# First expert layer: expert rows added to the tokens by indirect accumulating DMA in DRAM in place of one-hot products

## The chip, the cores and the metric

The kernel runs on one core of a Trainium2 chip. The metric is the device time of one execution in microseconds (us), and the median of several runs counts. A core has TensorE (PE, with its weight loads shown apart as PEld), VectorE (DVE), ScalarE (ACT), GpSimd (POOL) and SyncE (SP). DMAs are issued here from SP's and POOL's queues.

## The reference, cut to what matters

512 tokens of width 1024 (and 256 context tokens) go through a first block and then two layers, each a mixer followed by an expert layer with 16 experts. The change is in the first of the two expert layers, which serves both token sets. Every expert chooses its best tokens: 64 of the 512 tokens, 32 of the 256 context tokens. A token may be chosen by several experts, and their outputs are added.

```python
cap = max(1, EC_FACTOR * T // N_EXPERTS)              # 64 for tokens, 32 for the context
aff = softmax(h @ router)
gate, idx = lax.top_k(swapaxes(aff, 1, 2), cap)
xs = h[idx]
hid = silu(xs @ w1) * (xs @ w3)                       # per expert, 1024 x 1024 weights, float32
ys = (hid @ w2) * gate
out = zeros((T, D)).at[idx].add(ys)                   # x = x + g2 * out
```

## The kernel before

The function `moe` builds one expert layer. In the first layer it has two groups: group 0, the four token tiles of 128 x 1024 (`xres`), with 64 rows to an expert, and group 1, the two context tiles (`cres`), with 32 rows. 128 rows are handled together: two experts of group 0 (`ne` = 2), four of group 1 (`ne` = 4). So group 0 has 8 such bundles and group 1 has 4. The second expert layer has one group only (`alone`).

`choose` finds the chosen tokens on VectorE, eight at a time. `fetch` (L1479 to L1489) turns slot numbers into token numbers with one-hot products on TensorE: 4 of them for group 0 and 2 for group 1, each recorded as two instructions with 128 stationary columns. The token numbers (`ii`) drive an indirect gather on POOL's queue (L1483), which reads rows of the normalised tokens `xh` from DRAM into `xs`. `turn` (L1573 to L1579) transposes them.

`run` loops over the 16 experts. Of an expert, `up` (L1623) multiplies the rows of group 0 (`h`) and group 1 (`hc`) with w1 and w3, `act` and `turned` (L1630 to L1646) apply the gate and transpose, `down` (L1662) multiplies with w2 (`yb`), and `collect` (L1675 to L1680) puts the rows into `ys`. Twelve weight tiles of 1 MB serve one expert; 14 of them fit, and each is loaded on SP's queue (L1464) when the tile that held its place is free.

When a bundle's last expert is done, `scatter` is put into the list `beside`. Its steps run during the next expert: two of them between quarters of `up`, the rest after `act` of group 0. So group 0's scatter runs during experts 2, 4, 6, ... 14, group 1's during experts 4, 8 and 12, and the last scatter of each group after expert 15. `fetch` for the next bundle of group 0 stands in experts 0, 2, ... 12, that for group 1 in 2, 6 and 10, and `turn` an expert later.

A scatter of this layer scales the 128 rows by the gate on ACT (L1594, `yh` in a reduced matmul type, with the remainder `yl` from DVE, L1596). For every token tile it builds a one-hot matrix `back` on DVE (L1600), multiplies it with both halves of `yh` and `yl` on TensorE (L1605), and adds the product to the tile on DVE (L1607). That is 16 products for group 0, 8 for group 1. Group 1's rows are multiplied by the modulation gate on POOL first (L1593).

The order of instructions on each engine is fixed when the kernel is built, by a planner that follows the program order as a priority and its own estimates of times. Every engine runs its instructions in that order; a DMA's wait stands on the queue of the engine that issues it.

Of the kernel before, what the change touches and what calls it, by code (L numbers as in the profile page):

```python
# [10 lines left out]
F32 = mybir.dt.float32  # L11
F32R = mybir.dt.float32r
BF16 = mybir.dt.bfloat16
I32 = mybir.dt.int32
AF = mybir.ActivationFunctionType
ALU = mybir.AluOpType
# [4 lines left out]
D = 1024  # L21
# [1416 lines left out]
def moe(k, layer, groups, mods, psum, es, nslot, extra, out=None, side="right"):  # L1438
# [4 lines left out]
    nc, I = k.nc, k.i  # L1443
    bank = lambda nm="ps": psum.tile([128, 512], F32, name=nm, tag="ps")
    dp = k.pool(f"md{layer}", 1, DRAM, es)
    parts = [("w1", 0), ("w3", 0), ("w1", 1), ("w3", 1), ("w1", 2), ("w3", 2), ("w1", 3), ("w3", 3), ("w2", 0), ("w2", 1), ("w2", 2), ("w2", 3)]
    todo = [(e, nm, q) for e in range(16) for nm, q in parts]
    W, pools, G, made = {}, [], [], {}

    alone = len(groups) == 1  # L1450

    def slots():

        if not pools:
            pools.append(k.pool(f"mw{layer}", 1, None, es, side))
        return lambda: pools[0].tile([128, 2 * D], F32, name="w", tag="w", bufs=nslot)

    def load(upto, eng=nc.sync):

        for i in range(len(W), min(upto, len(todo))):  # L1460
            e, nm, q = todo[i]
            a = i % (nslot + extra) >= nslot
            w = pools[a].tile([128, 2 * D], F32, name="w", tag="w", bufs=extra if a else nslot).rearrange("p (k f) -> p k f", k=2)
            d = eng.dma_start(w, I[f"moe_{nm}_2"][layer, e][q * 256:q * 256 + 256].rearrange("(k p) f -> p k f", p=128))  # L1464
            if i < nslot + extra:
                k.tc.keep_in_program_order(d)
            W[e, nm, q] = w

    def fetch(g, gi, a):

        n, ne, cap = g["n"], g["ne"], g["cap"]
        b = bank()
        w = 1 if alone else n
        for t in range(0, n, w):
            oh = pf.tile([128, w, ne, cap], F32, name="oh", tag=f"oh{gi}", bufs=1 + alone)
            nc.vector.tensor_tensor(oh, iota[:, :cap].unsqueeze(1).unsqueeze(1).to_broadcast([128, w, ne, cap]),
                                    g["pos"][:, t:t + w, a * ne:a * ne + ne].unsqueeze(3).to_broadcast([128, w, ne, cap]), op=ALU.is_equal)
            for i in range(w):
                nc.tensor.matmul(b[:, :ne + 1], oh[:, i].rearrange("p e c -> p (e c)"), g["ext"][:, t + i, a], start=(t + i == 0), stop=(t + i == n - 1))  # L1479
        ii = pf.tile([128, 1], I32, name="ii", tag=f"ii{gi}", bufs=2)  # L1480
        nc.vector.tensor_copy(ii, b[:, 0:1])
        xs = pf.tile([128, D], F32, name="xs", tag="xs", bufs=len(groups))
        nc.gpsimd.indirect_dma_start(out=xs, out_offset=None, in_=g["xh"][:, :],  # L1483
                                     in_offset=bass.IndirectOffsetOnAxis(ap=ii[:, 0:1], axis=0))
        sl = pf.tile([128, ne + 1], F32, name="sl", tag=f"sl{gi}", bufs=2)
        nc.vector.tensor_copy(sl, b[:, :ne + 1])  # L1486
        gate = pf.tile([128, 1], F32, name="gt", tag=f"gt{gi}", bufs=2)
        for e in range(ne):
            nc.vector.tensor_scalar(gate[e * cap:e * cap + cap], sl[e * cap:e * cap + cap, 1 + e:2 + e], 0.5, None, ALU.mult)  # L1489
        return dict(xs=xs, sl=sl, gate=gate)  # L1490

    def begin(p):

# [87 lines left out]
    def scatter(g, c, last):  # L1581

        ys = c["ys"]
        last = last and out is not None
        dt = F32 if alone else F32R
        if alone:
            terms = [ys]
        else:
            terms = [p.tile([128, D], F32R, name=nm, tag=nm, bufs=1) for nm in ("yh", "yl")]
        pieces = [slice(0, 512), slice(512, 1024)] if last else [slice(0, D)]  # L1590
        for cs in pieces:
            if g["cap"] == 32:
                nc.gpsimd.tensor_tensor(ys, ys, g["gate"], op=ALU.mult)  # L1593
            nc.scalar.activation(terms[0][:, cs], ys[:, cs], AF.Copy, scale=c["gate"])  # L1594
            if not alone:
                nc.vector.scalar_tensor_tensor(terms[1][:, cs], ys[:, cs], c["gate"], terms[0][:, cs].bitcast(F32), ALU.mult, ALU.subtract)  # L1596
            yield
            for t in range(g["n"]):
                back = pf.tile([128, 128], dt, name="back", tag="back", bufs=2)
                nc.vector.tensor_scalar(back, iota, 128.0 * t, c["sl"][:, 0:1], ALU.add, ALU.is_equal)  # L1600
                for o in range(cs.start, cs.stop, 512):
                    hs = slice(o, o + 512)
                    b = bank()
                    for i, y in enumerate(terms):
                        nc.tensor.matmul(b, back, y[:, hs], start=(i == 0), stop=(i == len(terms) - 1))  # L1605
                    x = g["tiles"][t][:, hs]
                    nc.vector.tensor_tensor(x, x, b, op=ALU.add)  # L1607
                    if last:
                        nc.sync.dma_start(out[t * 128:t * 128 + 128, hs], x)
                if t % 2:  # L1610
                    yield
# [70 lines left out]
    def run():  # L1682
        nonlocal rp, pf, pq, p, iota, tid, one, hb
        slots()
        rp = k.pool(f"mr{layer}", 1, None, es)
        iota = rp.tile([128, 128], F32, name="iota")
        nc.gpsimd.iota(iota, pattern=[[1, 128]], base=0, channel_multiplier=0, allow_small_or_imprecise_dtypes=True)
        tid = rp.tile([128, 6], F32, name="tid")
        nc.gpsimd.iota(tid, pattern=[[128, 6]], base=0, channel_multiplier=1, allow_small_or_imprecise_dtypes=True)
        for gi, g in enumerate(G):  # L1690
            g["gate"] = mods.gate(g["r"], 1, rp, f"g2{layer}{gi}")
        if extra:
            pools.append(k.pool(f"mv{layer}", 1, None, es))
        load(nslot + extra - (2 if extra else 6))
        pf = k.pool(f"mf{layer}", 1, None, es)
        with ExitStack() as e2:
            pq = k.pool(f"mq{layer}", 1, None, e2, "left")
            one = pq.tile([16, 512], F32, name="one")
            nc.gpsimd.memset(one, 1.0)
            chosen = [choose(gi, g) for gi, g in enumerate(G)]  # L1700
            while any(g is None for g in nxt):
                for c in chosen:
                    next(c, 0)
        load(nslot + extra, nc.gpsimd)
        load(24)
        p = k.pool(f"mx{layer}", 1, None, es)
        for gi, g in enumerate(G):
            turn(g, gi, nxt[gi])
        for e in range(16):
            load(12 * e + 36)  # L1710
            for gi, g in enumerate(G):
                if e % g["ne"] == 0:
                    cur[gi] = nxt[gi]
            hb = [[bank("h1"), bank("h3")] if g["cap"] == 64 else [bank("hc")] for g in G]
            ybs, hTs, late = [bank("yb") for _ in G], [None] * len(G), len(G) - 1

            def ups(q, gi):
                if 0 <= q < 4:
                    up(e, q, gi, G[gi])

            def downs(q, gi):
                if 0 <= q < 4:
                    down(e, q, gi, G[gi], hTs[gi], ybs[gi])


            for q in range(4):
                ups(q, 0)
                if late:
                    ups(q - 1, 1)
                if q > 1:  # L1730
                    beside.step()
            th = act(0, G[0])
            beside.drain()
            for gi, g in enumerate(G):
                if e % g["ne"] == g["ne"] - 2 and e < 16 - 2:
                    nxt[gi] = fetch(g, gi, e // g["ne"] + 1)
            hTs[0] = turned(0, G[0], th)
            if late:
                ups(3, 1)
                th = act(1, G[1])  # L1740
            for q in range(4 + 2 * late):
                downs(q, 0)
                if late and q == 1:
                    hTs[1] = turned(1, G[1], th)
                if late:
                    downs(q - 2, 1)
                if q == 1:
                    for gi, g in enumerate(G):
                        if e % g["ne"] == g["ne"] - 1 and e < 15:
                            turn(g, gi, nxt[gi])  # L1750
            for gi, g in enumerate(G):
                collect(e, gi, g, ybs[gi])
                if e % g["ne"] == g["ne"] - 1:
                    beside.add(scatter(g, cur[gi], e == 15))
        beside.drain()
        es.close()
# [898 lines left out]
```

## Time and profile before

| | us |
|---|---|
| median of 3 runs | 3433.63 |
| lowest and highest | 3430.89, 3440.51 |
| the profiled execution's own time | 3434.85 |
| its span in the profile | 3432.6 |

The mean granted clock of TensorE over the span was 0.939 of full speed. PE was busy for 3083.4 us (90% of the span), DVE 1528.3, ACT 1014.2, POOL 976.9. The first expert layer's loop lies between 1497 and 2128 us of the span. What lies outside the span in the profiled execution is 2.25 us.

### The profile page before, as it was taken

Reading aid. Unit: us, or ns where it says so; the run is one execution under the profiler, and the core shown is the slowest. Engines: PE = TensorE matmul, PEld = TensorE weight load, DVE = VectorE, ACT = ScalarE, POOL = GpSimd, SP = SyncE. Lnnn points to the kernel's source line nnn. Section 1 sums busy time; section 2 is a strip of 40 time slices with the busy share of each in tenths; the row PEclk is TensorE's granted clock in tenths of the full one; section 3 lists DMA queues with packets and bytes.
Section 4 is the critical chain, followed back from the end, with each engine's and each line's share of the span. In section 5 each row is a group of like instructions: output and inputs, shape, how many; then the busy total and the mean of one; then the engine's idle time right before and its main releaser. Section 6 shows DMA issues by size and latency. Waiting matters only on the chain.

```text
span 3432.6 us, 52377 instructions
## 1 busy us (share of the span) xinstructions
PE 3083.4 (90%) x21072; PEld 2017.0 (59%) x21072; DVE 1528.3 (45%) x3435; ACT 1014.2 (30%) x2175; POOL 976.9 (28%) x859
## 2 busy tenths in 40 slices
PE   8999999999899889969999998899768579699888
PEld 6897878877668666833333333787547467333322
DVE  4324354423477786332323225321678776322212
ACT  4434333321213555211212112122647443011000
POOL 5342433433323561310000001424646343000000
PEclk9999999999999999979999999899879779799999
DMA  4121221235266331379888883343312234899998
GB/s 145 63 73 62 74 74 62 74 102 160 80 166 170 97 102 50 124 287 348 326 337 327 334 337 131 111 137 105 93 47 75 65 94 155 323 409 409 409 409 347
DMA packets 372551, 625.93 MB, mean 182 GB/s; under 512 B 43998, under 2 KB 240525, under 8 KB 372310
## 3 DMA queue, kind: packets, MB, share of 16 engines
q1 hardware_dynamic: 367190, 603.58, 49.3%
q0 software_dynamic: 5120, 19.01, 1.5%
q8 instruction: 166, 2.72, 0.3%
q14 instruction: 75, 0.61, 0.1%
HBM read 596.61 MB, written 25.91 MB: 181 GB/s over the span
## 4 chain that ended last, share of the span: by engine, by line
PE 73%; DVE 11%; DMA 8%; ACT 4%; issue 2%; POOL 2%; SPq 1%; DVEq 0%; ACTq 0%; POOLq 0%
PE ps L102 11%; PE h L1623 10%; PE ps L103 10%; PE ps L104 10%; PE yb L1662 7%; DMA w<-in_moe_w_dram 5%; PE hc L1623 4%; PE ps L1605 2%; PE ps L932 1%; PE ps L2259 1%; DVE pr L2314 1%; DVE acc L1106 1%; PE ob L1309 1%; DVE N L2315 1%; PE ps L1271 1%
## 5 line engine op out<-in xcount | busy, mean ns | idle before, releaser
L201 POOL TENSOR_TENSOR wlo<-wraw,whi 128x1024 fp32r<-128x1024 f32 (+5 forms) x219 | 426.0, 1967 | 734.0 <-ACT whi L197 708.9
L1623 PE MATMUL h<-w,xT 128*64 128x512 f32 x2048 | 463.8, 599 | 23.9 <-DMA w<-in_moe_w_dram 18.4
L1623 PEld LDWEIGHTS h<-w,xT 128*64 128x64 f32 x2048 | 141.3, 137 | 336.3 <-issue 254.1
L1662 PE MATMUL yb<-w,hT 128*64 128x512 f32 (+1 forms) x1536 | 301.6, 600 | 17.8 <-ACT hT L1646 15.4
L197 ACT CAST whi<-wraw 128x2048 fp32r<-128x2048 f32 (+4 forms) x108 | 161.7, 1497 | 233.0 <-PE ps L103 124.3
L1483 POOL DMA_INDIRECT xs<-xh,ii x20 | 21.4, 1069 | 733.4 <-DVE sl L1486 713.0
L1631 DVE SCALAR_TENSOR_TENSOR th<-th,h 128x512 f32<-128x512 f32 x32 | 22.0, 689 | 413.9 <-ACT th L1630 413.9
L1662 PEld LDWEIGHTS yb<-w,hT 128*64 128x64 f32 (+1 forms) x1536 | 87.3, 128 | 198.3 <-issue 155.7
L102 PE MATMUL ps<-hT,whi 128*128 128x512 f32 x416 | 171.2, 411 | 0.0
L102 PE MATMUL ps<-whi,hT 128*128 128x512 f32 (+1 forms) x424 | 163.3, 386 | 6.2 <-DVE hT L316 4.0
L1630 ACT ACTIVATE th<-h 128x512 f32<-128x512 f32 x32 | 19.1, 598 | 500.7 <-PE h L1623 500.7
L104 PE MATMUL ps<-hT,whi 128*128 128x512 f32 x416 | 166.1, 399 | 0.0
L103 PE MATMUL ps<-hT,wlo 128*128 128x512 f32 x416 | 166.1, 399 | 0.0
L103 PE MATMUL ps<-whi,hT 128*128 128x512 f32 (+1 forms) x424 | 155.7, 367 | 0.0
L104 PE MATMUL ps<-wlo,hT 128*128 128x512 f32 (+1 forms) x424 | 154.2, 366 | 0.0
L115 POOL TENSOR_TENSOR rs<-rs_t,mhalf 128x8 f32<-128x8 f32 (+3 forms) x78 | 96.0, 1235 | 119.2 <-DVE rs_t L110 99.6
L1675 DVE TENSOR_TENSOR ys<-yb,g 64x512 f32<-64x512 f32 x64 | 44.1, 689 | 180.2 <-PE yb L1662 179.6
L1623 PE MATMUL hc<-w,xT 128*32 128x512 f32 x1024 | 124.2, 598 | 0.0
L102 PEld LDWEIGHTS ps<-whi,hT 128*128 128x128 f32 x424 | 104.1, 246 | 15.7 <-DVE hT L316 4.3
L103 PEld LDWEIGHTS ps<-whi,hT 128*128 128x128 f32 x424 | 104.6, 247 | 6.5 <-issue 2.1
L1106 DVE SCALAR_TENSOR_TENSOR acc<-glu,w,acc 128x798 f32<-128x798 f32 x90 | 106.7, 1221 | 1.0
L104 PEld LDWEIGHTS ps<-wlo,hT 128*128 128x128 f32 x424 | 103.7, 245 | 5.4 <-issue 0.6
(810 smaller groups left out, 6787.7 us busy)
## 6 DMA issues: line engine op xcount, KB each, us to landing
w<-in_moe_w_dram SPq DMA_DIRECT2D x376, 1024.0 KB
wraw<-in_w_in_dram SPq DMA_DIRECT2D x48, 1024.0 KB
aw<-in_ada_w_dram SPq DMA_DIRECT2D x192, 256.0 KB
wraw<-in_od_w_in_dram SPq DMA_DIRECT2D x27, 512.0 KB
rows<-rw_rows SPq DMA_DIRECT2D x48, 192.0 KB
w<-in_moe_w_dram POOLq DMA_DIRECT2D x8, 1024.0 KB, 8.7
xh<-xn SPq DMA_DIRECT2D x10, 512.0 KB
wraw<-in_w_proj_b_dram SPq DMA_DIRECT2D x4, 1024.0 KB
```

The source lines that it names most:

```text
L102: nc.tensor.matmul(out, L[0], R[0], start=start, stop=False)
L103: nc.tensor.matmul(out, L[1], R[0], start=False, stop=False)
L104: nc.tensor.matmul(out, L[0], R[1], start=False, stop=stop)
L115: nc.gpsimd.tensor_tensor(out, t, mh.to_broadcast(list(ss.shape)), op=ALU.pow)
L197: nc.scalar.copy(hi, raw)
L201: eng.tensor_tensor(lo[:, a:b], raw[:, a:b], hi[:, a:b].bitcast(F32), op=ALU.subtract)
L932: nc.tensor.matmul(ps[32 * j:32 * j + 32, h * w:h * w + w], k.cT[:, 4 * q + j], raws[i][:, j], start=(q == 0), stop=(q == 1), tile_positio ...
L1106: v.scalar_tensor_tensor(acc[:, c], glu[:, c, j:j + W], w2[:, j, c:c + 1], acc[:, c], ALU.mult, ALU.add)
L1605: nc.tensor.matmul(b, back, y[:, hs], start=(i == 0), stop=(i == len(terms) - 1))
L1623: nc.tensor.matmul(bb[o:o + cap], lhs, w[:, kk % 2, fh * 512:fh * 512 + 512], start=(kk == 0), stop=(kk == 7), tile_position=(0, o))
L1662: nc.tensor.matmul(yb[o:o + cap], lhs, w[:, j, dh * 512:dh * 512 + 512], start=first, stop=last, tile_position=(0, o))
L1675: nc.vector.tensor_tensor(ys[so, ds_], yb[64 * dh:64 * dh + 64], g["gate"][so, ds_], op=ALU.mult)
```

## The change

In the first expert layer a copy of the tokens (`acc`, one per group) is written to DRAM when `run` begins, by six DMAs of 512 KB on SP's queue. `scatter` of every bundle but each group's last scales the rows once on ACT into a float32 tile `yd` (one buffer for both groups) and issues one indirect accumulating DMA per expert on POOL's queue, 64 or 32 rows of 4 KB each, which adds the rows to `acc` at the token numbers. When one bundle of a group is left, the tiles are read back from `acc` on SP's queue. The last bundle of each group goes back by one-hot products as before. An indirect DMA takes its row numbers from the first partitions on, so `fetch` makes the token numbers of a bundle's second and later experts once more, by further products with one column on the cap partitions, and copies them to `i2`.

```diff
@@ fetch
+            if not alone:
+                for e in range(1, ne):
+                    for i in range(n):
+                        nc.tensor.matmul(b[:cap, 8 + e:9 + e], oh[:, i, e], g["ext"][:, i, a, 0:1], start=(i == 0), stop=(i == n - 1))
-        ii = pf.tile([128, 1], I32, name="ii", tag=f"ii{gi}", bufs=2)
+        ii = pf.tile([128, 1], I32, name="ii", tag=f"ii{gi}", bufs=2 if alone else 3)
         nc.vector.tensor_copy(ii, b[:, 0:1])
+        own = [ii[:cap]]
+        if not alone:
+            i2 = pf.tile([cap, ne], I32, name="i2", tag=f"i2{gi}", bufs=3)
+            nc.vector.tensor_copy(i2[:, 1:], b[:cap, 9:8 + ne])
+            own += [i2[:, e:e + 1] for e in range(1, ne)]
@@ scatter
+        g["left"] -= 1
+        if g["left"] and not alone:
+            if g["cap"] == 32:
+                nc.gpsimd.tensor_tensor(ys, ys, g["gate"], op=ALU.mult)
+            y = p.tile([128, D], F32, name="yd", tag="yd", bufs=1)
+            nc.scalar.activation(y, ys, AF.Copy, scale=c["gate"])
+            yield
+            for e in range(g["ne"]):
+                so = slice(e * g["cap"], e * g["cap"] + g["cap"])
+                nc.gpsimd.indirect_dma_start(out=g["acc"][:, :], out_offset=bass.IndirectOffsetOnAxis(ap=c["own"][e], axis=0),
+                                             in_=y[so], in_offset=None, compute_op=ALU.add)
+            yield
+            if g["left"] == 1:
+                for t, x in enumerate(g["tiles"]):
+                    nc.sync.dma_start(x, g["acc"][t * 128:t * 128 + 128])
+            return
@@ run
+        for gi, g in enumerate(G):
+            g["left"] = 16 // g["ne"]
+            if not alone:
+                g["acc"] = dp.tile([g["n"] * 128, D], F32, name=f"acc{gi}")
+                for t, x in enumerate(g["tiles"]):
+                    nc.sync.dma_start(g["acc"][t * 128:t * 128 + 128], x)
```

## Rows read from the trace of the kernel before

**Rows 1.** The page: the 40 slices, and the chain that ended last.
```profile
PE   8999999999899889969999998899768579699888
PEclk9999999999999999979999999899879779799999
GB/s 145 63 73 62 74 74 62 74 102 160 80 166 170 97 102 50 124 287 348 326 337 327 334 337 131 111 137 105 93 47 75 65 94 155 323 409 409 409 409 347
...
PE 73%; DVE 11%; DMA 8%; ACT 4%; issue 2%; POOL 2%; SPq 1%; DVEq 0%; ACTq 0%; POOLq 0%
```
**Rows 2.** Stretches: busy time per engine, clock, DMA share, GB/s; whole experts, a pause.
```profile
1760.00:1800.00 40.00, 39.33 (x230) 13.00 (x227) 7.35 (x13) 7.05 (x15) 0.00 (x0) 1.00 0.86 333
...
1840.00:1842.00 2.00, 2.00 (x12) 0.77 (x12) 0.00 (x0) 0.37 (x1) 0.00 (x0) 1.00 0.00 0
```
**Rows 3.** Waits of SP's queue, 1400 to 2135 us: total, times, longest.
```profile
SPq L1464 <- PE hc L1623: 335.9, 61, 52.4
SPq L1464 <- PE yb L1662: 202.8, 58, 16.3
```
**Rows 4.** PE in order of time: first products of experts 2, 14, 15; what follows 15.
```profile
1570.35 7.09 PE L1623 MATMUL h<-w,xT 128*64 128x512 f32 x32
...
2039.49 7.09 PE L1623 MATMUL h<-w,xT 128*64 128x512 f32 x32
...
2078.50 7.09 PE L1623 MATMUL h<-w,xT 128*64 128x512 f32 x32
...
2113.32 1.21 PE L1605 MATMUL ps<-yh,back 128*128 128x512 f32 x4
```
**Rows 5.** PE in order of time: transposes of one bundle, of two.
```profile
1721.09 1.09 PE L1573 MATMUL ps<-cc,xs 128*128 128x128 f32 x8
...
1797.15 1.97 PE L1573 MATMUL ps<-cc,xs 128*128 128x128 f32 x16
```
**Rows 6.** Groups of the stage by shape, 1497 to 2128 us.
```profile
L1605 PE MATMUL ps<-yh,back 128*128 128x512 f32 x80 | 32.5, 430 | 9.1 <-ACT yh L1594 6.3 <-DVE back L1600 2.7
L1605 PE MATMUL ps<-yl,back 128*128 128x512 f32 x80 | 32.0, 435 | 1.5 <-DVE yl L1596 1.5
...
L1479 PE MATMUL ps<-ext,oh 128*128 128x3 f32 x56 | 7.1, 249 | 0.0
```
**Rows 7.** PE in order of time, expert 2: fetch products and transposes.
```profile
1596.04 1.40 PE L1479 MATMUL ps<-ext,oh 128*128 128x3 f32 x12
1597.29 0.63 PE L1645 MATMUL ps<-cc,th 128*128 128x128 f32 x4
1598.60 6.22 PE L1662 MATMUL yb<-w,hT 128*64 128x512 f32 x26 [0.68 <-ACT hT L1646]
```
**Rows 8.** PE in order of time, expert 10: the same products as rows 7's third.
```profile
1911.27 7.92 PE L1662 MATMUL yb<-w,hT 128*64 128x512 f32 x26 [0.67 <-ACT hT L1646]
```
**Rows 9.** Stretches of 2 us in experts 4, 8 and 10; the clock is third from last.
```profile
1678.00:1680.00 2.00, 2.00 (x7) 1.06 (x7) 1.65 (x6) 0.59 (x1) 0.84 (x1) 0.57 1.01 346
...
1834.00:1836.00 2.00, 2.00 (x6) 0.96 (x6) 1.96 (x7) 0.41 (x1) 0.96 (x1) 0.50 1.02 393
...
1912.00:1914.00 2.00, 2.00 (x6) 0.48 (x4) 1.24 (x9) 0.00 (x0) 1.70 (x2) 0.50 1.02 395
```
**Rows 10.** PE in order of time: group 0's first fetch, and expert 0's first products.
```profile
1486.57 1.84 PE L1479 MATMUL ps<-ext,oh 128*128 128x3 f32 x8 [1.14 <-DVE oh L1476]
...
1497.15 7.89 PE L1623 MATMUL h<-w,xT 128*64 128x512 f32 x32
```
**Rows 11.** SP's queue in order of time: the first weight loads.
```profile
1445.84 72.87 SPq L1464 DMA_DIRECT2D w<-in_moe_w_dram  x14
```
**Rows 12.** The tile xs in the stage: its gathers' landing times.
```profile
DMA to landing us min/median/max: 5.7/6.0/8.5
```
**Rows 13.** ACT in order of time, expert 4: the scalings of group 0 and group 1.
```profile
1645.72 1.15 ACT L1594 ACTIVATE yh<-ys,gt 128x1024 fp32r<-128x1024 f32 x1 [0.27 <-DVE ys L1675]
...
1673.00 1.15 ACT L1594 ACTIVATE yh<-ys,gt 128x1024 fp32r<-128x1024 f32 x1 [1.22 <-PE ps L1605]
```

More of the change, by code (lines that the diff above doesn't have):

```diff
@@ L1489, in fetch @@
             nc.vector.tensor_scalar(gate[e * cap:e * cap + cap], sl[e * cap:e * cap + cap, 1 + e:2 + e], 0.5, None, ALU.mult)
-        return dict(xs=xs, sl=sl, gate=gate)
+        return dict(xs=xs, sl=sl, gate=gate, own=own)
     def begin(p):
```

## Prediction

> **What bounds the kernel now.** I read the page first. The chain that ended last is PE for 73%, and among the 40 slices six stand out, from the nineteenth on: PE busy 90% or more, the clock nearly full, and 326 to 348 GB/s, while the second expert layer moves 409 GB/s at the end of the kernel [rows 1]. So the first expert layer may be bound by PE or by its weights, and the second view, stretches, has to say which. One expert without a scatter shows PE busy for 39.33 of 40 us at full clock with the DMA engines at 0.86; and late in expert 8 there are 2 us in which PE is busy throughout and the DMA engines move nothing [rows 2]. SP's queue says why: the weight loads waited 335.9 + 202.8 us for PE to free a tile [rows 3]. All 14 weight tiles were full; PE sets the pace. What leaves PE in this stage comes off the end, as long as the weights keep up.
>
> How much PE time is the scatter's? The third view is PE in order of time. Expert 15 has neither scatter, fetch nor turn and takes 2113.32 - 2078.50 = 34.82 us. Expert 14 has group 0's scatter alone and takes 2078.50 - 2039.49 = 39.01 [rows 4], so one such scatter costs 4.19. The 13 experts from 2 to 14 take 2078.50 - 1570.35 = 508.15 us, or 55.5 over 13 x 34.82. Turns are 8.8 of it: in three odd experts 16 transposes and in three 8, about 1.9 and 1.0 each by their lengths less the 0.07 by which neighbours overlap [rows 5]. 46.7 us are left for the seven even experts: seven scatters of group 0, three of group 1, and six fetches with 24 + 36 instructions.
>
> **The change part by part.** *Scatter removed.* The old fetch products stay: 12 of them took 1597.29 - 1596.04 = 1.25 us [rows 7], 0.104 each, so 60 of them 6.2. The scatters are the other 40.5. As a second way to it: 136 of the 160 products go, and the groups sum to 64.5 us for all 160, in which neighbours overlap [rows 6]; at expert 14's 4.19 for 16, 136 would be 35.6. The further 5 us are waits, and the three places where the clock fell, with a granted clock of 0.50 to 0.57, the level of 1.2 GHz, in experts 4, 8 and 10 [rows 9]. One fall costs what the same 26 products took more in expert 10 than in expert 2: 7.92 - 6.22 = 1.7 us [rows 8, 7]. I take 40.5 off. Bounds: 35.6 and 40.5.
>
> *Products added to fetch.* Each fetch of group 0 gets 4 more products, 8 instructions; each of group 1 gets 6, 12 instructions. In the loop that is 7 x 8 + 3 x 12 = 92 instructions, all on PE's path. They stream one column, with 64 or 32 stationary columns. The trace has no such shape; the nearest are the old fetch products with their 128 stationary columns at 0.104 us [rows 7]. I take 0.10, near that row: 9.2 us. Bounds: 0, if they vanish between their neighbours, and the group's busy time per instruction, 7.1 / 56 = 0.127 [rows 6], 11.7 us.
>
> The Trainium skill ("TensorE: Matmul & The Clock Gate", Part 2, on loading the stationary operand) makes a weight load cost columns / 1.2 ns. For 128 columns that is 107 ns, and the row above agrees with 104. By that rule 64 and 32 columns would cost 53 and 27 ns, the 92 instructions 3.9 us in place of 9.2, and the sum would be 5.3 us lower.
>
> *Clock.* The 20 added instructions in experts 2, 6 and 10 lengthen a stretch that already ends in a wait of 0.67 us for `hT`, and in expert 10 the clock fell right there [rows 8, 9]. In experts 4, 8 and 12 the wait for `yh` that stood before the falls goes away. I take 4 falls in the seven fetch places, 6.8 us. Bounds: none, and all seven, 11.9.
>
> *Start of the layer.* Before expert 0 the fetch products run at 1.84 / 8 = 0.23 us [rows 10]. Group 0's 8 further ones delay its gather: 1.8 us. Group 1's 12 delay only the copy to `ii`, behind which VectorE's search for group 0 is queued; 2.8 if VectorE must wait for all of it, nothing if its order lets it go on. I take 1.0. Together 2.8; bounds 1.8 and 4.6. The six copies to `acc` on SP's queue go ahead of the first weights: 3.1 MB at 333 GB/s [rows 2], 9 us. Of those weights eight are issued from 1445.84 on [rows 11], and by that rate have landed at about 1471; 1480 with the copies ahead of them, while the first product with weights starts at 1497.15 [rows 10]. What hides the copies is the search for the tokens; without it they would cost 9. I take nothing.
>
> *ACT, DVE and POOL.* One scaling stays on ACT. DVE loses `back`, `yl` and the additions, and gains copies of a few columns. Neither is on the chain in this stage. POOL gets 26 accumulating DMAs. Each changes the same tensor as the one before it, so each must wait on POOL's queue until that has landed. Behind them on that queue stand group 1's multiplication and the next gathers. The nearest row is the gather, 128 rows in 5.7 to 8.5 us, median 6.0 [rows 12]. I call one accumulate's landing time L and take 6; it moves half the rows, but must read them before it writes. Bounds: 3, half a gather, and 17, twice the slowest.
>
> With L = 6, `yd`, shared by both groups, is free again two landings after group 0's scaling, 12 us later, while group 1's scaling came 1673.00 - 1645.72 = 27.3 us later [rows 13]. So ACT doesn't wait.
>
> *Reading back.* Four 512 KB loads in expert 14 and two in expert 12 wait on SP's queue for the last accumulate, and weight loads may stand behind them. 13 free tiles are 13 x 34.82 / 12 = 37.7 us of lead; the wait is at most 2L = 12 us and 6L = 36 us. Nothing, though just so.
>
> *Sum:* -40.5 + 9.2 + 6.8 + 2.8 = -21.7. The profiled execution's 3434.85 becomes 3413.2. It stands 1.2 us over the median, so the median should be 3412.
>
> **The rivals.** *Late gathers (slower).* In experts 4, 8 and 12 POOL issues two accumulates for group 0, a multiplication, and four for group 1, then group 0's gather. From the scaling on this gather is issued after about 5L + 3 and lands after 5L + 9. PE needs it at the turn, 1721.09 - 1647 less 5.5 for the work that has left, 68.6 us [rows 5, 13]. From L = 11.9 us on PE waits, three times 5 us for each us of L; at L = 11.9 + 21.7 / 15 = 13.4 the gain is gone, and at 17 the kernel takes 3412 + 76 = 3488. For it: an accumulate reads and writes, and no row shows one. Against it: half the rows of a gather that never took over 8.5.
>
> *The weights become the bound.* An expert's 12.58 MB in 34.82 us are 361 GB/s. A stretch at 0.86 share moved 333 [rows 2], so a full one 387. The loop took 2113.32 - 1497.15 = 616.2 us [rows 4, 10] and is to take 616.2 - 40.5 + 9.2 + 6.8 = 591.7; 178 of the 192 weight tiles are loaded within it, so in about 549 us of it. They are 187 MB; with 5.2 MB accumulated and 3.1 MB read back that is 505 us at 387. If an accumulated byte costs as much as four plain ones it is 545 and still hidden; at six the gain is gone, and at eight, 599 us, the kernel is 28 us slower, 3462. For it: each accumulate moves its bytes at least twice. Against it: the pauses in which all tiles are full.
>
> *Only the scatter counts.* The added products cost a third of what I took, the clock doesn't fall, and the start costs its lower bound: -40.5 + 3.1 + 1.8 = -35.6, 3398. For it: three of the six even experts with a fetch kept the clock. Against it: PE was busy in 39.33 of 40 us and hides nothing.
>
> *The gain is eaten.* All bounds go wrong together: -35.6 + 11.7 + 11.9 + 4.6 = -7.4, 3426; or the planner reorders work around the change and a wait of one expert grows by 3 us in seven experts, and there is no change.
>
> **How the numbers follow.** The forecast, 3402 to 3421, has 0.62. Only the scatter counts: 0.13. The gain largely eaten, 3421 to 3432: 0.10, with a third of it within 0.3% (10 us, about what a measurement of this kernel tells from no change). Weights: 0.05, one in five of it slower, the rest faster by less. Late gathers: 0.10, of which 0.07 slower, 0.02 the same and 0.01 faster. So faster 0.87, same 0.05, slower 0.08. The range that leaves out no more than 2 in 10: 3396 to 3430.
>
> **What would show it.** L1605 falls from 160 products to 24; even experts shrink, expert 14 to 34.8 us, expert 2 to about 38, expert 4 to about 37. L1479 has 92 further instructions in the loop; their spacing is the second term. Two-microsecond stretches after the fetches tell the falls of the clock. The accumulates' landing time is L; PE's wait for `xs` in experts 5, 9 and 13 must stay empty. SP's queue must still wait for PE above all. The prediction is wrong if PE begins to wait for a DMA in this stage, or if the stage outside the loop changes its length by more than 5 us.

## The result, and the profile after

| | before | after |
|---|---|---|
| median | 3432.26 us (4 runs) | 3392.23 us (4 runs) |
| lowest, highest | 3430.65, 3440.51 | 3389.09, 3395.77 |
| profiled execution: own time, span | 3434.85, 3432.6 | 3395.77, 3394.0 |

The ratio is 0.9882, with a 95% interval of 0.9866 to 0.9899. The change gains 40.0 us by the medians and 38.6 by the spans; forecast were 21.7, with 3396 to 3430 as the range. The sign was right, the size was not.

The page of the kernel after: what the DMAs moved in the 40 slices, and the chain that ended last.

```profile
GB/s 146 63 75 63 75 67 71 63 87 174 81 167 181 92 97 57 83 300 369 369 379 361 359 380 136 130 129 89 98 52 73 66 90 156 350 409 409 409 409 347
...
PE 73%; DVE 11%; DMA 8%; ACT 4%; issue 2%; POOL 2%; SPq 0%; ACTq 0%; DVEq 0%; POOLq 0%
```

Against [rows 1] the first expert layer moves 359 to 380 GB/s in place of 326 to 348: the same weights in less time. PE still makes up 73% of the chain. What SP's queue waited for between 1400 and 2097 us says that PE still sets the pace:

```profile
SPq L1464 <- PE hc L1648: 335.8, 60, 50.4
SPq L1464 <- PE yb L1687: 161.2, 55, 11.7
SPq L1607 <- DMA acc<-yd,i: 27.9, 1, 27.9
```

The first wait is as long as in [rows 3], the second a fifth shorter (161.2 us against 202.8). The new one, 27.9 us before the token tiles are read back, stands behind the last weight load of that queue and stops nobody: no engine waited for `xres` or `cres`. (Lines have moved: up is L1648, down L1687, the one-hot products L1630, the old fetch products L1479, the new ones L1483, the accumulates L1602.)

The groups of the stage from 1500 to 2090 us, and the time from an accumulate's issue to its landing:

```profile
L1602 POOL DMA_INDIRECT acc<-yd,i x16 | 21.7, 1356 | 73.2 <-DMA acc<-yd,ii 44.3 <-DMA acc<-yd,i 28.4 <-issue 0.6
L1602 POOL DMA_INDIRECT acc<-yd,ii x10 | 14.1, 1410 | 277.8 <-ACT yd L1598 277.6 <-issue 0.2
L1598 ACT ACTIVATE yd<-ys,gt 128x1024 f32<-128x1024 f32 x10 | 11.5, 1148 | 3.6 <-DVE ys L1700 2.1 <-DMA acc<-yd,i 1.4
...
L1630 PE MATMUL ps<-yh,back 128*128 128x512 f32 x12 | 5.1, 514 | 4.9 <-ACT yh L1619 3.2 <-DVE back L1625 1.7
...
L1483 PE MATMUL ps<-ext,oh 128*64 128x1 f32 x56 | 4.4, 200 | 0.0
```
```profile
DMA to landing us min/median/max: 4.7/6.8/9.8
```

The one-hot products have gone from 160 to 24 instructions, 12 of each half. POOL waits for one accumulate before it issues the next, and ACT waits for `yd` 1.4 us in the whole stage.

PE in order of time in expert 2, which answers [rows 7]:

```profile
1589.92 1.94 PE L1648 MATMUL hc<-w,xT 128*32 128x512 f32 x16
1591.78 1.05 PE L1479 MATMUL ps<-ext,oh 128*128 128x3 f32 x8
1592.77 0.63 PE L1483 MATMUL ps<-ext,oh 128*64 128x1 f32 x8
1593.32 0.61 PE L1479 MATMUL ps<-ext,oh 128*128 128x5 f32 x4
1593.86 0.54 PE L1483 MATMUL ps<-ext,oh 128*32 128x1 f32 x12
1594.33 0.65 PE L1670 MATMUL ps<-cc,th 128*128 128x128 f32 x4
1594.92 1.94 PE L1648 MATMUL hc<-w,xT 128*32 128x512 f32 x16
1596.79 7.09 PE L1687 MATMUL yb<-w,hT 128*64 128x512 f32 x32
...
1604.72 3.64 PE L1687 MATMUL yb<-w,hT 128*32 128x512 f32 x32 [0.46 <-ACT hT L1671]
```

Two things differ from [rows 7] besides the new rows. Behind the transposes of `th` stands the last quarter of group 1's products with w1 and w3 (`hc`, 16 instructions, 1.94 us). While PE works on it, ACT copies `hT`, and the wait of 0.68 us for `hT` is gone. And the 32 products `yb` that follow run without a break at full clock.

The experts' lengths, from first product to first product, experts 0 to 15:

```
before 37.36 35.84 40.22 36.72 43.55 35.85 40.22 36.71 43.57 35.84 41.91 36.72 41.99 35.84 39.01 34.82
after  35.70 35.85 36.30 36.71 35.30 35.84 36.30 36.72 35.29 35.84 37.95 36.72 35.29 35.84 34.82 34.82
```

The loop's length is 616.2 us before and 575.3 after, 40.9 less. Expert 14 is as short as expert 15. Experts 4, 8 and 12, with a fetch of group 0, take 0.48 us more than expert 15, and 2 and 6, with both fetches, 1.48. Expert 10 takes 37.95, because the clock fell there once, behind the fetch (third from last: 0.50, the level of 1.2 GHz):

```profile
1884.00:1886.00 2.00, 2.00 (x13) 0.24 (x4) 0.00 (x0) 0.00 (x0) 1.69 (x2) 0.50 1.01 414
```

### The profile page after: what moved, and what is told of

It reads as the page before. It is cut to its first block, busy times and chain, and to the rows that moved or that the text cites. A ratio compares the mean times of both kernels' runs of the same rounds, so it can differ in the third digit from the quotient of the medians.

```text
span 3394.0 us, 52291 instructions
## 1 busy us (share of the span) xinstructions
PE 3046.7 (90%) x21048; PEld 1994.9 (59%) x21048; DVE 1472.5 (43%) x3335; ACT 1013.1 (30%) x2175; POOL 1014.0 (30%) x885
## 4 chain that ended last, share of the span: by engine, by line
PE 73%; DVE 11%; DMA 8%; ACT 4%; issue 2%; POOL 2%; SPq 0%; ACTq 0%; DVEq 0%; POOLq 0%
PE ps L102 11%; PE h L1648 11%; PE ps L103 10%; PE ps L104 10%; PE yb L1687 7%; DMA w<-in_moe_w_dram 6%; PE hc L1648 4%; PE ps L932 1%; PE ps L1630 1%; DVE pr L2345 1%; PE ps L1271 1%; PE ob L1309 1%; DVE acc L1106 1%; DVE N L2346 1%; PE lb L1532 1%
## 5 line engine op out<-in xcount | busy, mean ns | idle before, releaser
L1648 PE MATMUL h<-w,xT 128*64 128x512 f32 x2048 | 463.4, 598 | 22.5 <-DMA w<-in_moe_w_dram 17.0
L1648 PEld LDWEIGHTS h<-w,xT 128*64 128x64 f32 x2048 | 141.2, 137 | 334.6 <-issue 248.6
L1687 PE MATMUL yb<-w,hT 128*64 128x512 f32 (+1 forms) x1536 | 296.1, 596 | 19.5 <-ACT hT L1671 16.1
L1687 PEld LDWEIGHTS yb<-w,hT 128*64 128x64 f32 (+1 forms) x1536 | 86.5, 128 | 199.2 <-issue 153.8
L1648 PE MATMUL hc<-w,xT 128*32 128x512 f32 x1024 | 123.5, 604 | 0.0
```

What stands on the lines that cost most here:

```text
L1648: nc.tensor.matmul(bb[o:o + cap], lhs, w[:, kk % 2, fh * 512:fh * 512 + 512], start=(kk == 0), stop=(kk == 7), tile_position=(0, o))
L1687: nc.tensor.matmul(yb[o:o + cap], lhs, w[:, j, dh * 512:dh * 512 + 512], start=first, stop=last, tile_position=(0, o))
```

## The experiments

The loop below is the time from the first product of expert 0 to the end of expert 15's last one, from each kernel's profile, so from one execution each. The kernels ran in groups, each beside the kernel before on its own chip; the ratio is against those runs.

| kernel | median, us | ratio, 95% interval | loop, us |
|---|---|---|---|
| before | 3432.26 | | 616.2 |
| after | 3392.23 | 0.9882 [0.9866, 0.9899] | 575.3 |
| no_scatter | 3386.99 | 0.9880 [0.9859, 0.9901] | 574.6 |
| no_extra | 3389.56 | 0.9882 [0.9863, 0.9900] | 575.4 |
| extra_alone | 3442.32 | 1.0030 [1.0015, 1.0045] | 626.0 |
| extra_twice | 3400.46 | 0.9920 [0.9900, 0.9941] | 585.8 |
| hc_first | 3399.18 | 0.9898 [0.9877, 0.9918] | 586.2 |
| turn_first | 3395.00 | 0.9881 [0.9864, 0.9898] | 573.5 |
| acc_twice | 3420.42 | 0.9958 [0.9946, 0.9971] | 593.3 |
| acc_twice_two_yd | 3436.95 | 1.0009 [0.9996, 1.0022] | 607.1 |
| twelve | 3398.00 | 0.9887 [0.9872, 0.9902] | 586.0 |
| all_dma | 3402.38 | 0.9908 [0.9890, 0.9926] | 577.3 |
| pin_up | 3377.94 | 0.9830 [0.9815, 0.9845] | 563.5 |
| pin_up_twice | 3396.20 | 0.9886 [0.9862, 0.9909] | 562.4 |

**The parts one by one.** no_scatter is the kernel before without the one-hot scatters, but for each group's last:

```diff
+        g["left"] = g.get("left", 16 // g["ne"]) - 1
+        if g["left"] and not alone:
+            return
```

> The kernel before with every scatter but each group's last left out, so those rows never reach the tokens: no one-hot products, no accumulating DMA, no copies. Theory A: the scatters and what they disturb are worth more than the 40.5 us that I took off, about 42 to 44 in the loop, since the old fetch products are hidden too once the scatters are gone; 3388 to 3391 us. Theory B: 40.5 us in the loop, 575.7, and what the changed kernel adds costs nothing.

no_extra is the kernel after without the added products; the accumulates of a bundle's later experts take the first expert's row numbers:

```diff
-                for e in range(1, ne):
-                    for i in range(n):
-                        nc.tensor.matmul(b[:cap, 8 + e:9 + e], oh[:, i, e], g["ext"][:, i, a, 0:1], start=(i == 0), stop=(i == n - 1))
...
-            own += [i2[:, e:e + 1] for e in range(1, ne)]
+            own += [ii[:cap]] * (ne - 1)
```

> The changed kernel without the added products in fetch and without their copy to i2; the rows of a bundle's later experts are added at the first expert's token numbers, so the sums differ from the reference. Theory A: the added products (5.3 us of PE time by their spacing in the changed kernel) mostly fill gaps in which PE waited for hT anyway; the loop, 575.3 us in the changed kernel, shrinks by 0.5 to 3 us and the kernel takes 3388 to 3392 us. Theory B, as predicted: every added product lies on the path, at 0.10 us for each of 92 and with falls of the clock; the loop shrinks by 9 us or more, and the kernel takes about 3382.

extra_alone is the kernel before with the added products (and the copy to `i2`, which nobody uses), scatters as before:

> The kernel before with the added products in fetch and their copy to i2 and nothing else of the change; the scatters stay one-hot products. Theory A: the products cost at most their spacing, 5.3 us, less what falls into gaps, and hardly a fall of the clock more: +2 to +6 us, 3434 to 3438 us. Theory B: +9.2 us and four falls of 1.7 us, with the start 2.8: +16 to +19, 3449 us.

By the loops: without the scatter 616.2 goes to 574.6, so the scatter was worth 41.5 us there. With the accumulates and the read-back put in, 575.4: 0.7 more. With the added products as well, 575.3: nothing net, although under both expectations the loop of no_extra was to shrink. The experts one by one show what the sums hide:

```
no_scatter 36.55 35.85 35.09 36.72 36.55 35.85 35.09 36.72 36.55 35.84 35.09 36.72 36.55 35.84 34.82 34.82
no_extra   37.23 35.84 35.09 36.72 36.55 35.84 35.09 36.72 36.55 35.84 35.09 36.72 36.55 35.90 34.82 34.82
```

Between these two nothing but expert 0 differs by more than 0.1 us, and its 0.68 lies in its first products, long before the first accumulate: in the loop the accumulates cost nothing. The added products then make experts 2, 6 and 10 longer by 1.21 us each, with the fall of the clock on top in expert 10; but experts 4, 8 and 12 become 1.26 shorter and expert 0 1.53. PE in expert 4 of no_extra, and then of the kernel after:

```profile
1661.72 1.90 PE L1642 MATMUL hc<-w,xT 128*32 128x512 f32 x6
1663.56 0.66 PE L1664 MATMUL ps<-cc,th 128*128 128x128 f32 x4
1664.14 1.92 PE L1642 MATMUL hc<-w,xT 128*32 128x512 f32 x10
1665.99 7.09 PE L1681 MATMUL yb<-w,hT 128*64 128x512 f32 x32
```
```profile
1665.79 0.63 PE L1483 MATMUL ps<-ext,oh 128*64 128x1 f32 x8
1666.34 0.66 PE L1670 MATMUL ps<-cc,th 128*128 128x128 f32 x4
1666.93 1.94 PE L1648 MATMUL hc<-w,xT 128*32 128x512 f32 x16
```

In no_extra the planner put the transposes into the last quarter of group 1's products. The two parts of 6 and 10 instructions take 1.84 and 1.85 us from start to start, and the whole quarter takes 1.87: the cut costs 1.8 us. With the 8 added products, 0.55 us, the quarter stays whole. no_scatter has the same cut in experts 0, 4, 8 and 12, the kernel before in expert 0. So the added products weren't free. They cost about 5.8 us (three times 1.21, four times 0.55), the fall 1.65 more, and four cuts fewer gave about as much back.

In the same way the 41.5 of no_scatter holds three new cuts. In the order of the kernel after, the removal is worth more: without the added products its even experts from 2 to 14 would take three times 35.09, three times 34.73 (36.55 less the cut) and 34.82, 244.3 us against 290.5 before. By this estimate the scatter was worth 46.2 us.

Added to the kernel before, the 92 instructions made the loop 9.8 us longer, and the kernel slower by 0.3%, which lies between the two expectations. In experts 4 and 8, where the clock falls once in both kernels, 8 of them cost 0.60 us. The rest is a wait and falls of the clock, less 1.9 in expert 0, whose quarter they left whole. PE in expert 2 of extra_alone, and then two of its stretches of 2 us (the clock is third from last):

```profile
1593.56 0.95 PE L1479 MATMUL ps<-ext,oh 128*128 128x3 f32 x8
1594.43 0.63 PE L1483 MATMUL ps<-ext,oh 128*64 128x1 f32 x8
...
1596.00 1.11 PE L1652 MATMUL ps<-cc,th 128*128 128x128 f32 x4
1597.79 6.11 PE L1669 MATMUL yb<-w,hT 128*64 128x512 f32 x16 [0.68 <-ACT hT L1653]
```
```profile
1594.00:1596.00 2.00, 2.00 (x29) 1.94 (x29) 2.00 (x6) 0.26 (x1) 0.00 (x0) 0.99 0.87 342
1596.00:1598.00 2.00, 1.32 (x9) 0.92 (x8) 1.97 (x11) 0.59 (x1) 1.23 (x1) 0.50 1.01 395
```

There the fetch runs straight into the transposes, PE waits 0.68 us for `hT`, and the clock goes down to 0.50, the level of 1.2 GHz. It fell in all six experts with a fetch from 2 to 12, against three in the kernel before; summed over stretches of 1 us, 15.3 us of clock were missing in the loop against 5.1, some of it while PE waited. In expert 2 the kernel after has the fetch, the transposes and then a quarter of long products, and the clock stays up:

```profile
1592.00:1594.00 2.00, 2.00 (x24) 1.95 (x24) 0.57 (x4) 0.00 (x0) 0.14 (x1) 1.00 1.04 418
...
1596.00:1598.00 2.00, 2.00 (x14) 0.48 (x8) 0.41 (x1) 0.59 (x1) 0.46 (x1) 1.00 1.04 416
```

extra_twice issues the added products of each fetch twice:

```diff
-                for e in range(1, ne):
+                for e in [*range(5, 4 + ne), *range(1, ne)]:
                     for i in range(n):
-                        nc.tensor.matmul(b[:cap, 8 + e:9 + e], oh[:, i, e], g["ext"][:, i, a, 0:1], start=(i == 0), stop=(i == n - 1))
+                        nc.tensor.matmul(b[:cap, 8 + e:9 + e], oh[:, i, (e - 1) % 4 + 1], g["ext"][:, i, a, 0:1], start=(i == 0), stop=(i == n - 1))
```

> The changed kernel with each added product of fetch issued twice, the second time into unused columns. Theory A: another 5.3 us of PE time in the loop, of which less fits into gaps than of the first: +2 to +6 us over the changed kernel, and one to three falls of the clock. Theory B: +9 us and falls in all of experts 2, 6 and 10 at the least, +14 to +20.

The loop grew by 10.5 us: 92 more instructions at the spacing of expert 2's rows (8 with 64 columns from 1592.77 to 1593.32, 69 ns each; 12 with 32 columns from 1593.86 to 1594.33, 39 ns each) are 56 x 0.069 + 36 x 0.039 = 5.3 us, and the clock fell four times in place of once, 6.8 us lost in place of 1.7. Where the clock didn't fall, 8 more of them cost 0.47 us (expert 12) and 20 more 0.84 (experts 2 and 6). Products behind the fetch cost their spacing here too; 10.5 us lies between the two expectations.

**The place of the quarter.** hc_first takes group 1's last quarter out from behind the transposes and puts it ahead of the fetch, in every expert; PE's work is otherwise the same:

```diff
+            if late:
+                ups(3, 1)
             for gi, g in enumerate(G):
                 if e % g["ne"] == g["ne"] - 2 and e < 16 - 2:
                     nxt[gi] = fetch(g, gi, e // g["ne"] + 1)
             hTs[0] = turned(0, G[0], th)
             if late:
-                ups(3, 1)
                 th = act(1, G[1])
```

> The changed kernel with the last quarter of group 1's up products moved ahead of the fetch in program order; on PE the 16 hc instructions then stand before the fetch products and the transposes instead of behind them, and nothing else differs. Theory A: the products of fetch were free because those 16 hc instructions behind the transposes covered the copy of hT and kept PE dense; without them each fetch costs its PE time, 1.5 or 2.5 us, the wait for hT of 0.7 us comes back and the clock falls in three or more of the seven places: loop 582 to 593 us, kernel +7 to +18. Theory C: they are free wherever they stand: within 1 us.

Its expert 2:

```profile
1590.38 3.66 PE L1648 MATMUL hc<-w,xT 128*32 128x512 f32 x32
1593.97 1.05 PE L1479 MATMUL ps<-ext,oh 128*128 128x3 f32 x8
...
1596.52 0.66 PE L1670 MATMUL ps<-cc,th 128*128 128x128 f32 x4
1597.85 3.65 PE L1687 MATMUL yb<-w,hT 128*64 128x512 f32 x16 [0.68 <-ACT hT L1671]
```

The wait of 0.68 us is back, and the loop is 10.9 us longer than in the kernel after: four falls of the clock in place of one (5.1 us more), without a fall 1.07 us more in an expert with one fetch (36.36 against 35.29) and 0.22 in one with both (36.52 against 36.30), and 0.8 more at the start of expert 0. So the place of 16 instructions is worth some 10 us of the loop, as expected. The kernels' ratios don't tell the two apart (0.9898 and 0.9882, with overlapping intervals), and the falls are those of one execution.

turn_first goes the other way: group 1's last quarter stays behind the transposes in the odd experts too.

```diff
-                    nc.tensor.matmul(bb[o:o + cap], lhs, w[:, kk % 2, fh * 512:fh * 512 + 512], start=(kk == 0), stop=(kk == 7), tile_position=(0, o))
+                    mm = nc.tensor.matmul(bb[o:o + cap], lhs, w[:, kk % 2, fh * 512:fh * 512 + 512], start=(kk == 0), stop=(kk == 7), tile_position=(0, o))
+                    if gi and q == 3:
+                        k.tc.keep_in_program_order(mm)
```

> The changed kernel with the last quarter of group 1's up products pinned behind the transposes of group 0 in every expert, so that the nine experts without a fetch get the order that the experts with one have. Theory A: those nine experts lose their wait for hT and shrink by 0.3 to 0.7 us each; loop 569 to 573 us, kernel 3386 to 3390 us. Theory C: PE waits for the gate chain ahead of the transposes in place of hT, no change.

The odd experts up to 13 became 1.6 us shorter, as expected, but experts 14 and 15 became 3.2 and 2.5 us longer, and the clock fell twice; the loop missed its range by 0.5 us and the kernel by 5. PE waits for nothing more in expert 14 and keeps its clock; its products are cut up:

```profile
2001.77 1.91 PE L1648 MATMUL hc<-w,xT 128*32 128x512 f32 x6
...
2021.05 1.94 PE L1648 MATMUL hc<-w,xT 128*32 128x512 f32 x16
```

A whole quarter of group 1, 16 instructions, takes 1.94 us. Six of them, cut off by products of group 0, take 1.91. The planner had mixed the groups, and PE was busy throughout for less work.

pin_up therefore holds the products with w1 and w3 of both groups in program order:

```diff
+                    if not alone:
+                        k.tc.keep_in_program_order(mm)
```

> The first products (w1, w3) of both groups in this layer are held in program order on TensorE, so that no expert mixes or splits a group of them, and every expert makes the transposes of th before the last quarter of group 1's products. Theory (placement: a quarter of group 1's products behind the transposes covers the copy to hT, and group 1's groups kept whole are what the run with the transposes first lacked): the seven odd experts up to 13 and experts 14 and 15 take about 1.6 us less each (34.2 to 35.1, and 33.2), the fetch experts stay at 35.3 to 36.3, the loop takes 559 to 564 us in place of 575.3, and the kernel 3376 to 3382. Rival (what the other order gained by its mixing is lost when the products are held, or the waits move elsewhere): loop 572 to 580, kernel 3389 to 3397. Rival (PE gets ahead of its weights): PE waits for w, SP's queue no longer waits for PE above all.

3377.94 us, 0.9830 of the kernel before. Expert 1 of pin_up, and then of the kernel after (pin_up's lines stand two later from L1649 on):

```profile
1549.88 1.94 PE L1648 MATMUL hc<-w,xT 128*32 128x512 f32 x16
1551.74 0.66 PE L1672 MATMUL ps<-cc,th 128*128 128x128 f32 x4
1552.33 1.94 PE L1648 MATMUL hc<-w,xT 128*32 128x512 f32 x16
1554.20 7.09 PE L1689 MATMUL yb<-w,hT 128*64 128x512 f32 x32
...
1562.63 3.64 PE L1689 MATMUL yb<-w,hT 128*32 128x512 f32 x32
```
```profile
1554.07 3.66 PE L1648 MATMUL hc<-w,xT 128*32 128x512 f32 x32
1557.67 0.66 PE L1670 MATMUL ps<-cc,th 128*128 128x128 f32 x4
1559.00 7.08 PE L1687 MATMUL yb<-w,hT 128*64 128x512 f32 x30 [0.68 <-ACT hT L1671]
...
1567.42 4.64 PE L1687 MATMUL yb<-w,hT 128*64 128x512 f32 x34
```

The odd expert loses the wait of 0.68 us, and 1.0 us in the last row, where the kernel after had kept the last two instructions of group 0 apart from their group. Seven odd experts gain 1.6 each, experts 14 and 15 1.1 and 1.5, and one more fall of the clock gives 1.7 back: 11.8 us off the loop. The kernel gains 14 us by the medians; of the spans' 17.2, 3.7 lie behind the stage and 4.4 before its loop, where nothing was changed, and the end of the stage gives 2.7 back, where DVE waited for `xres`.

**The rivals: accumulates, weights, read-back.** acc_twice issues each accumulate twice:

```diff
-            for e in range(g["ne"]):
+            for e in [e for e in range(g["ne"]) for _ in range(2)]:
```

> The changed kernel with each accumulating DMA issued twice in a row, so the rows are added twice and the sums differ from the reference. The time of a chain of accumulates doubles, as with L = 14. Late gathers, as the prediction priced them: PE waits about 10 us for xs in experts 5, 9 and 13, +30 us. Rival: the planner put group 0's gather ahead of group 1's accumulates, so no gather waits; 0 to +3 us. Rival on bandwidth: the DMA engines, at 0.96 of their time in the loop now, have no room for 5.2 MB more of accumulates, and PE waits for weights: +5 to +15.

The loop grew by 18.0 us and the end of the stage by 10, together nearly what late gathers were to cost. But it wasn't late gathers: PE waited 1.5 us for `xs`, in expert 9. In expert 10 ACT, then PE:

```profile
1891.84 1.15 ACT L1598 ACTIVATE yd<-ys,gt 128x1024 f32<-128x1024 f32 x1 [13.68 <-DMA acc<-yd,i]
```
```profile
1884.17 3.42 PE L1648 MATMUL hc<-w,xT 128*32 128x512 f32 x16
1898.57 8.54 PE L1687 MATMUL yb<-w,hT 128*64 128x512 f32 x32 [10.97 <-ACT hT L1671]
```

The scaling waits until the accumulates have read `yd`, which has one buffer; the copy to `hT` is queued behind it on ACT, PE waits for that, and the clock falls. acc_twice_two_yd gives `yd` a second buffer, with 13 weight tiles to make room:

```diff
-            y = p.tile([128, D], F32, name="yd", tag="yd", bufs=1)
+            y = p.tile([128, D], F32, name="yd", tag="yd", bufs=2)
```

> Each accumulating DMA is issued twice, so the rows are added twice and the output differs from the reference; yd has two buffers in place of one, and the weights 13 tiles in place of 14, to make room. Theory (the doubled accumulates cost 18 us only because ACT's next scaling waits until yd's DMAs have landed, and the copy to hT is queued behind it on ACT): ACT waits for DMA less than 3 us in the stage in place of 25, PE's waits for hT go back to about 10 us, loop 576 to 581 us in place of 593.3, kernel 3393 to 3399. Rival (the doubled traffic or the queue of POOL itself is what costs): loop 588 to 596, kernel 3414 to 3422. Rival (gathers come late): PE waits for xs in experts 5, 9 and 13 by more than 5 us each.

ACT no longer waited for a DMA there, and up to expert 8 every expert is as long as in the kernel after. Yet the loop grew to 607.1, and none of the three expectations came: from expert 9 on the planner, with other estimates, cut group 1's products up as in turn_first (experts 12 to 15: 40.1, 42.3, 41.3 and 40.5 us). twelve, the kernel after with 12 weight tiles in place of 14, shows the same on a smaller scale.

> Only the number of weight tiles of the first expert layer changes, 12 in place of 14. Theory (PE sets the pace with a margin, weights are loaded an expert ahead): loop 575 to 577.5 us, kernel 3390 to 3395, no wait of PE for w. Rival (the weights have become the bound or nearly so, since the DMA engines are now at a share of 0.92 to 1.0): PE waits for w, most of all in experts 4, 8, 12 and 14, and the loop takes over 580 us, kernel over 3397.

PE didn't wait for `w`. Experts 13 to 15 are 8.7 us longer with cut-up groups, and the clock fell twice in place of once. The rival's number came out and its mechanism didn't.

pin_up_twice puts the doubled accumulates, two buffers of `yd` and 13 tiles into pin_up:

> The run with the up products held, with each accumulating DMA issued twice (so the rows are added twice and the output differs from the reference), two buffers of yd and 13 weight tiles. PE's order is that of the run with the up products held, so this is what twice as many accumulates cost when neither a scaling waits for yd nor a group of products is broken up. Theory (the accumulates cost nothing, the 18 and 35 us of the two runs before were the wait for yd and the broken groups of group 1's products): each of group 1's groups takes 1.9 us for 16 instructions, no wait for xs or w over 2 us in the loop, loop 563 to 569 us against 563.5, kernel 3378 to 3385. Rival (the doubled traffic slows the weights, or the gathers come late): PE waits for w or xs, loop over 575 us, kernel over 3390.

The loop takes 562.4 us against 563.5, or 0.6 more than pin_up's once the fall of the clock that it has fewer (1.7) is put back. 45 of the 52 accumulates landed in it: there they cost next to nothing, and PE's waits for `w`, its weight loads' with them, add up to 0.3 us. The kernel is nevertheless 18 us slower than pin_up, and the place is the end of the stage. PE there, and SP's queue:

```profile
2088.75 0.77 PE L1630 MATMUL ps<-yh,back 128*128 128x512 f32 x1 [13.18 <-DVE xres L1632]
```
```profile
2084.53 1.75 SPq L1607 DMA_DIRECT2D xres<-acc  x4
```

The accumulates go one behind the other, and the last seven land after the loop. The token tiles are read back when the last has landed, 25 us after the loop's end, and the last one-hot scatter needs them. From the loop's end to the next stage PE takes 33.4 us, in pin_up 16.8. all_dma sends the last bundles that way too:

```diff
-        if g["left"] and not alone:
+        if not alone:
...
-            if g["left"] == 1:
+            if g["left"] == 0:
```

> The changed kernel with the last bundle of each group going back by accumulating DMA too, and the tiles read back after it. Group 1's four accumulates come after group 0's two, 6 landings of 7 us and two loads, about 50 us after expert 15, where the one-hot products took 14; what follows can start with the token tiles. +10 to +35 us over the changed kernel. Rival: the next stage needs the context tiles late and hides most of it: +3 to +10.

It nearly keeps the loop (577.3) and pays at the end: from the loop's last product to the first one behind the stage PE is idle for 22.9 us, where the kernel after takes 14.1 with its scatters. The kernel is 10 us slower than the kernel after, where the two expectations meet.

## Why the prediction was wrong

**What bounds the stage: right.** SP's queue waited for PE as before, and pin_up, which only changes PE's order, took 11.8 us off the loop with the same weights.

**Scatter removed, -40.5: this step failed.** no_scatter's loop is 41.5 us shorter, but that agreement is luck: three new cuts in group 1's quarters are in it. In the order of the kernel after, the removal took about 46.2 us off the even experts, above the bounds of 35.6 and 40.5. The prediction left an even expert the length of expert 15 and the old fetch products, 34.82 + 1.25 = 36.07 us for expert 2; no_scatter shows 35.09. So with all terms expert 2 was to take about 38 us and took 36.30, and expert 4 35.30 in place of about 37. Expert 15 was the wrong measure, since it holds a wait for `hT` and keeps two instructions of group 0 apart from their group. PE in expert 15 of the kernel before:

```profile
2101.35 7.08 PE L1662 MATMUL yb<-w,hT 128*64 128x512 f32 x30 [0.68 <-ACT hT L1646]
...
2108.75 4.64 PE L1662 MATMUL yb<-w,hT 128*64 128x512 f32 x34
```

In the kernel after, the experts with a fetch have these 32 instructions together and a wait of 0.46 us in place of 0.68 (expert 2 above). The program has the fetch, the transposes and then group 1's last quarter. In the kernel before, the planner had drawn that quarter ahead, among the scatter's products, and [rows 7] show what was left, transposes and a wait. PE in expert 2 of the kernel before:

```profile
1592.20 1.94 PE L1623 MATMUL hc<-w,xT 128*32 128x512 f32 x16
1594.07 0.50 PE L1605 MATMUL ps<-yh,back 128*128 128x512 f32 x1
```

With the scatter gone the quarter stands where the program has it. The prediction named a planner that reorders the work, but as a loss alone. Expert 0, which has no scatter, became 2.2 us shorter besides, without its added products: 1.8 for the cut in its quarter and 0.4 for a shorter time at the low clock at its start. The prediction had nothing there.

**Products added to fetch, +9.2: on the path, as predicted, but too dear.** They cost about 5.8 us in the loop, 5.3 by their spacing. By an estimate from the Trainium skill's rule ("TensorE: Matmul & The Clock Gate", Part 2) they were 3.9, with 53 and 27 ns for 64 and 32 columns; the rows give 69 and 39, between the rule and my 0.10. That no_extra's loop is as long as the kernel's after doesn't make them free, and the 9.8 us of extra_alone don't confirm the 9.2: both sums hold the planner's other orders and falls of the clock.

**Clock, four falls, +6.8: this step failed.** One fall, in expert 10, cost 37.95 - 36.30 = 1.65 us, which confirms the price of 1.7. "A stretch that already ends in a wait of 0.67 us" was no longer there: hc_first, which restores it, has four falls, one of them in expert 0. Why it fell in expert 10 and not in 2 and 6, which have the same order, isn't settled; in twelve and all_dma it fell in 2 and 6.

**Start, +2.8: mis-sized.** From the transposes behind the search to group 0's first turn PE took 15.87 us before and 16.95 after, so 1.1 more; the copy of group 1 didn't hold up the search. A further 2.2 us had gone before these transposes. In the profiles of the kernels here they start between 1471.7 and 1480.1 us, and two kernels that both write `acc` first (extra_twice and acc_twice_two_yd) are at the two ends; so the 2.2 can't be put down to the change.

**The sum.** In the loop -46.2 for the scatter, -2.2 in expert 0, 5.8 for the products and 1.7 for the clock make -40.9, where -40.5 + 9.2 + 6.8 = -24.5 was forecast. Of the 16.4 between them the order behind the removal has 7.9 (with expert 0), the clock 5.1 and the price of the products 3.4. Outside the loop it was 1.1 + 2.2 less 1.1 behind it, 2.2 in place of 2.8.

**ACT, DVE, POOL, weights: nothing, right.** An accumulate landed in 6.8 us; 6 had been taken. ACT waited 1.4 us for `yd`. The rival of late gathers didn't come even with twice the accumulates, but for one wait of 1.5 us; what came first was the one buffer of `yd`, which the prediction had named and found free. The weights didn't become the bound even at twice the accumulated bytes.

**Reading back, "nothing, though just so": right, and as narrow as that.** In the kernel after no engine waited for it. In pin_up, with a shorter loop, DVE waited 2.7 us for `xres`; in pin_up_twice PE stood still for 13.2.

**Rivals.** "Only the scatter counts" (3398) came nearest. It had no fall and 3.1 us for the products, both too little, and the scatter's 40.5, also too little, so part of its nearness is luck.

## What to carry to other kernels

When a planner orders an engine's work, price an addition in the order that will stand after the removal: look in the program for work that the removed part had drawn ahead and that will come back to cover a wait. When two kernels take equally long, compare them part by part before calling what lies between them free: here 5.8 us of products and a fall of the clock hid behind four cuts that had gone. Then count PE's time by whole groups, since a group of products on narrow tiles that is cut by others costs nearly the same for a part as for the whole. And where rows go back by DMA, look at the end of the stage first: the accumulates were free in the loop as long as their source tile came free in time, and cost 3 to 17 us at its end wherever a reader stood close behind them.

## What the runs showed of the hardware

- Sixteen instructions on 32-column tiles, one behind the other, took 1.94 us; six of them between products of other tiles 1.91. PE was busy throughout in both.
- An indirect accumulating DMA of 64 or 32 rows of 4 KB landed in a median of 6.8 us (4.7 to 9.8) beside the weight loads, and twice as many of them made no expert of pin_up longer by more than 0.4 us.
- The DMA engines ran at a share of 1.04 (a transfer counts whole in the stretch in which it starts), with 416 and 418 GB/s, in the two stretches shown of expert 2, and PE's products there waited for no weight.
